# Two rows of a down-projection at once, a rotation product on another engine, and a fourth weight pair, in an encoder layer on one Trainium2 core

## The chip, the cores and the metric

The kernel runs on one core of one Trainium2 chip. The metric is the device time of one execution in microseconds (us); lower is better. A core has five engines that work side by side, each through its own queue in order: TensorE (PE in the profile, its weight loads PEld), VectorE (DVE), ScalarE (ACT), GpSimd (POOL) and SyncE (SP), which here only issues transfers.

## The reference

One layer of an encoder on 512 tokens of width 1024, all in 32-bit floats:

```python
def swiglu(x, w1, w3, w2):
    return (jax.nn.silu(x @ w1) * (x @ w3)) @ w2          # 1024 -> 2816 -> 1024

def layer(x):
    x = x + 0.5 * swiglu(rmsnorm(x, ffn1_norm), ...)
    h = rmsnorm(x, mix_norm)
    proj = h @ w_in                # queries, keys, values of attentions A and B, gates
    o_a = dilated attention of three head groups with a T5 position bias, merged
    q, k = rope(rmsnorm(q, q_norm)), rope(rmsnorm(k, k_norm))   # attention B, 8 heads of 128, 2 of k and v
    o_b = softmax(q @ k.T * scale) @ v
    x = x + (sigmoid(g_a) * (o_a @ P_a) + sigmoid(g_b) * (o_b @ P_b)) @ w_out
    x = x + 0.5 * swiglu(rmsnorm(x, ffn2_norm), ...)
    return rmsnorm(x, final_norm)

def apply_rope(x, cos, sin):       # on pairs of columns
    return x0 * c - x1 * s, x0 * s + x1 * c
```

## The kernel before

The activations lie transposed: 8 tiles of 128 features x 512 tokens (`x`). Each matmul of 32-bit numbers is made of three on split operands (`mm3`, L215 to L217): a high part `H` and a rest `L` of each side, as H·H, H·L and L·H. So each weight tile of 128x1024 is loaded by SP (`wr`, `wa`, `wt`), cast by ScalarE to its high part (`wh`, L200) and subtracted by VectorE for the rest (`wl`, L201): it is "split". The order in which all weight tiles are used is one list (`self.order`). Before each use, `weights` issues the loads and splits ahead of it, as far as buffers go: three pairs `wh`, `wl` (the ring "wh"), and, while a pool `self.wx` is open, a fourth pair (the ring "whx") for every fourth tile of some kinds. A pair is free again when TensorE has done its last matmul with it.

TensorE's instructions run in the order in which the code writes them (`manual_schedule`); the other engines' queues are put in order by the tile scheduler. A static queue runs in order on the chip, so a row that waits holds those behind it.

The stages that the change touches:

- *FFN* (`ffn_run`, twice, "a" and "b"). The hidden 22 tiles are made in three groups (8, 8, 6 columns of tiles) by a Strassen scheme, two tiles at a time; the last step of a pair is `A22`, then VectorE multiplies (`c`, L459, L460) and the result `gg` is cast (ScalarE, L424) and its rest formed (VectorE, L425). After each group comes a down-projection with `w2` (`blocks`): for each of 8 output rows, one bank of PSUM collects the products with all `gg` of the group (24 matmuls for eight, 18 for six), and is added to `x` (`add`, L479 and L480). Four banks `mm` go round. In the first group of the first FFN, `done` of rows 0 to 2 also calls `bias_rows`: SP loads `onehot` and `vmask` (one buffer each), TensorE makes a small product `bps` (L579), VectorE makes `v` (L580), and GpSimd writes it out.
- *Rope stage of attention B*. The projections ("b", 0), ("b", 1), ("b", 2) take four banks at once, one per 128 tokens, and use 12 weight tiles `wb`; gate row ("g", 8) stands between the last two. For each 128 tokens `rope` copies the bank (`xk`, ScalarE), squares it (`sqb`), sums (`ss`, VectorE) and gets 1/root (`ms`, VectorE; `rs`, GpSimd, L365); `turn`, one step later, scales `xk` (L910), forms the product with the cosines `xa` on VectorE (L911) and with the sines `xb` on GpSimd (L912), and combines them on VectorE (L913, L914). `rope_t` transposes `xk` on TensorE (`Tq`) for the attention, which follows with scores `Sb`, exponentials `Pb`, transposes `Tb` and `PTH`, `PTL`. A gate row leaves its bank through VectorE (`z`, L617).

Of the kernel before, what the change touches and what calls it, by code (L numbers as in the profile page):

```python
# [28 lines left out]
GAP_S = 2  # L29
GAP_B = 1  # L30
LAG = 1
T = 512
D = 1024
NK = 8
# [16 lines left out]
def tile_at(li):  # L51
    if li < 4:
        return 256 * li, (256 if li < 3 else 128), (0 if li < 3 else 64)
    return GP + 256 * (li - 4), 256, 256


def f32(t):
    return t.bitcast(F32)


class Layer:
# [123 lines left out]
    def prep(self):  # L185
        n = len(self.tiles)
        if n == len(self.order) or not (n in self.raws or self.kind[n] == "ws"):
            return False
        tag = "whx" if self.order[n][0][:2] in ("sw", "w2") and n % 4 == 3 and self.wx is not None else "wh"
        both = self.ring(tag, n, self.used, n)  # L190
        if both is None:
            return False
        name, key = self.order[n][:2]
        if n not in self.raws:
            self.load(n)
        raw, (H, L) = self.raws[n], both
        if name[:2] == "sw" and key[1] in ("S2", "S4"):
            a, b = (self.raws[self.index[name, (key[0], q)]] for q in (("S1", "A11") if key[1] == "S2" else ("S2", "A12")))
            self.nc.vector.tensor_add(raw, a, b)
        self.nc.scalar.copy(H, raw)  # L200
        self.nc.vector.tensor_sub(L, raw, f32(H))  # L201
        self.tiles.append(both)
        return True
# [123 lines left out]
        s = slice(128 * (n % 8), 128 * (n % 8) + 128)  # L327
        return self.cur[0][:, s], self.cur[1][:, s]

    def blocks(self, name, rows, n=0):  # L330
        for pairs, done in rows:
            ps = self.bank()
            for k, pair in enumerate(pairs):
                self.mm3(ps, *self.block(name, n), *pair, k == 0, k == len(pairs) - 1)
                n += 1
            done(ps)

    @staticmethod
    def weave(main, fill):
# [63 lines left out]
    def ffn_run(self, s, gin, gnext, hooks, out, side, gp):  # L403
        nc = self.nc
        g, t, c, half = [], {}, {}, []
# [96 lines left out]
        lo, n = first, 0  # L502
        for gi, hi in enumerate(ends):
            last = hi == NF
            for _ in self.strassen(s, range(lo, hi, 2), evict):
                for fn in late[:2]:
                    fn()
                del late[:2]

            def done(d, ps, gi=gi, last=last):  # L510
                down(d, ps, last)
                if (gi, d) in side:
                    side[gi, d]()

            rows = [(list(g), lambda ps, d=d: done(d, ps)) for d in range(NK)]
            if last and out is not None:
                break
            self.blocks("w2" + s, rows, n)
            n, lo = n + NK * len(g), hi
            g.clear()  # L520
        if out is None:
            return
        nf, half = len(g), NK // 2
        self.blocks("w2" + s, rows[:half], n)
        ws = [[self.block("w2" + s, n + d * nf + f) for f in range(nf)] for d in range(half, NK)]

        def norm(hf):
# [13 lines left out]
        for hf in range(2):  # L541
            cs = slice(256 * hf, 256 * hf + 256)
            for d in range(half, NK):
                ps = self.bank()
# [354 lines left out]
    def turn(self):  # L899
        if self.turned is None:  # L900
            return
        (grp, i, nh, xk, rs), self.turned = self.turned, None
        nc, bp = self.nc, self.bp
        GC, GS = self.tabs[1 if grp == 0 else 0]
        w = 128 * nh
        x4 = xk[:, :w].rearrange("p (h e d) -> p h e d", h=nh, e=2)
        bc = lambda t: t[:, i].unsqueeze(1).to_broadcast([128, nh, 2, 64])
        xa = bp.tile([128, 4, 2, 64], F32, tag="xa", name="xa", bufs=2)[:, :nh]
        xb = bp.tile([128, 4, 2, 64], F32, tag="xb", name="xb", bufs=2)[:, :nh]
        nc.vector.tensor_mul(x4, x4, rs[:, :nh].unsqueeze(2).unsqueeze(3).to_broadcast([128, nh, 2, 64]))  # L910
        nc.vector.tensor_mul(xa, x4, bc(GC))  # L911
        nc.gpsimd.tensor_mul(xb, x4, bc(GS))  # L912
        nc.vector.tensor_sub(x4[:, :, 0], xa[:, :, 0], xb[:, :, 1])  # L913
        nc.vector.tensor_add(x4[:, :, 1], xb[:, :, 0], xa[:, :, 1])  # L914
        self.roped[grp, i] = xk
# [64 lines left out]
    def mixer(self):  # L980
        nc, tc = self.nc, self.tc
# [6 lines left out]
        with tc.tile_pool(name="oA", bufs=1, reuse_waits="tile") as oa:  # L988
# [25 lines left out]
            with tc.tile_pool(name="B", bufs=1, reuse_waits="tile") as bp:  # L1014
                self.qH = bp.tile([128, 8, T], F32R, name="qH")
                self.qL = bp.tile([128, 8, T], F32R, name="qL")
                with tc.tile_pool(name="KV", bufs=1, reuse_waits="tile") as kv:
                    self.kH = kv.tile([128, 2, T], F32R, name="kH")
                    self.kL = kv.tile([128, 2, T], F32R, name="kL")
                    self.vH = kv.tile([128, 4, 256], F32R, name="vH")  # L1020
                    self.vL = kv.tile([128, 4, 256], F32R, name="vL")
                    with tc.tile_pool(name="Bp", bufs=1, reuse_waits="tile") as b2:
                        self.rope_tables(b2)
                        self.until(fill, ("b", 0))
                        self.weave(self.rope_t(0, 4, 4), fill)
                        self.until(fill, ("b", 1))
                        self.weave(self.rope_t(1, 6, 6), fill)
                        self.until(fill, ("b", 2))
                        self.weave(self.rope_t(2, 6, 4), fill)
                    with tc.tile_pool(name="Ba", bufs=2, reuse_waits="tile") as pp:  # L1030
                        self.weave(self.attn_b(pp), fill)
                for _ in fill:
                    pass
                self.hctx.close()
                with tc.tile_pool(name="M", bufs=1, reuse_waits="tile") as mp:
                    mH = [mp.tile([128, T], F32R, name=f"mH{d}") for d in range(NK)]
                    mL = [mp.tile([128, T], F32R, name=f"mL{d}") for d in range(NK)]
                    m = {}

                    def gate(j):  # L1040
                        z = mp.tile([128, T], F32, tag="z", name="zg", bufs=4)
                        nc.sync.dma_start(z, self.gate_d[j])
                        nc.scalar.activation(z, z, AF.Sigmoid, bias=self.par[:, G_BG + j:G_BG + j + 1])
                        return z

                    def done_a(d, ps):
                        m[d] = mp.tile([128, T], F32, tag="ma", name="ma", bufs=2)
                        nc.vector.tensor_mul(m[d], ps, gate(d))

                    def done_b(d, ps):  # L1050
                        z = gate(NK + d)
                        nc.vector.tensor_mul(z, ps, z)
                        nc.vector.tensor_add(z, z, m[d])
                        nc.scalar.copy(mH[d], z)
                        nc.vector.tensor_sub(mL[d], z, f32(mH[d]))

                    def done_o(d, ps):
                        nc.vector.tensor_add(self.x[d], self.x[d], ps)
                        self.norm_h(d, G_FFN2)
                        self.norm_sq(d)  # L1060

                    oa_p = list(zip(self.oH, self.oL))
                    ob_p = [(self.qH[:, k, :], self.qL[:, k, :]) for k in range(8)]
                    rows = []
                    for d in range(NK):
                        rows += [(oa_p, lambda ps, d=d: done_a(d, ps)), (ob_p, lambda ps, d=d: done_b(d, ps))]
                    self.blocks("wab", rows)
                    self.open_h()
                    mm = list(zip(mH, mL))
                    self.blocks("wo", [(mm, lambda ps, d=d: done_o(d, ps)) for d in range(NK)])  # L1070
# [64 lines left out]
    return w.reshape(k // 128, 128, n // 128, 128).transpose(2, 1, 0, 3).reshape(n // 128, 128, k)  # L1135


def block_chunks(w):
    k, n = w.shape
    b = w.reshape(k // 128, 128, n // 128, 128).transpose(2, 0, 1, 3).reshape(-1, 8, 128, 128)  # L1140
    return b.transpose(0, 2, 1, 3).reshape(-1, 128, 1024)


# [5 lines left out]
def arrange(inp):  # L1149
    p = {k: np.asarray(v) for k, v in inp.items()}  # L1150
    out = constants()
# [6 lines left out]
    half = np.concatenate([np.arange(0, 128, 2), np.arange(1, 128, 2)])  # L1158
    gqk = np.stack([p["q_norm"][0][half], p["k_norm"][0][half]]).reshape(1, 2, 2, 64)
    out["gqk"] = np.broadcast_to(gqk, (128, 2, 2, 64))  # L1160
    for s, n in (("a", 1), ("b", 2)):
        w1 = feat_chunks(p[f"ffn{n}_w1"][0])
        w3 = feat_chunks(p[f"ffn{n}_w3"][0])
        out["w13" + s] = np.stack([w1, w3], axis=1).reshape(2 * NF, 128, 1024)
        ends = (0,) + GROUPS[s][1:]
        w2 = p[f"ffn{n}_w2"][0]
        out["w2" + s] = np.concatenate([block_chunks(w2[128 * lo:128 * hi]) for lo, hi in zip(ends, ends[1:])])
    w = p["w_in"][0]
    wa = w[:, :4608].reshape(D, 3, 3, 512)
    qk = wa[:, 0:2].reshape(D, 2, 3, 4, 128)  # L1170
# [28 lines left out]
```

## Time and profile before

| | |
|---|---|
| median of 3 runs | 1311.01 us (1309.3 to 1313.32) |
| profiled execution | 1314.01 us, its span 1312.2 us |
| mean granted TensorE clock | 0.993 |
| TensorE, VectorE, ScalarE, GpSimd busy | 97%, 67%, 45%, 11% of the span |
| DMA | 181.91 MB, mean 139 GB/s |

A row of the profile's timeline reads: start in us from the span's start, duration in us, engine, line, operation, output<-inputs by the program's names, shapes, count, and in brackets the idle time of the engine before it with what ended that. Of a row in a view of waits: who waited <- for whom: us in total, times, the longest. A matmul's row lasts longer than the distance to the next, since they are pipelined; the distance of two starts is what one takes of the time.

### The profile page before, as it was taken

Reading aid. Unit: us, or ns where it says so; the run is one execution under the profiler, and the core shown is the slowest. Engines: PE = TensorE matmul, PEld = TensorE weight load, DVE = VectorE, ACT = ScalarE, POOL = GpSimd, SP = SyncE. Lnnn points to the kernel's source line nnn. Section 1 sums busy time; section 2 is a strip of 40 time slices with the busy share of each in tenths; the row PEclk is TensorE's granted clock in tenths of the full one; section 3 lists DMA queues with packets and bytes.
Section 4 is the critical chain, followed back from the end, with each engine's and each line's share of the span. In section 5 each row is a group of like instructions: output and inputs, shape, how many; then the busy total and the mean of one; then the engine's idle time right before and its main releaser. Section 6 shows DMA issues by size and latency. Waiting matters only on the chain.

```text
span 1312.2 us, 19971 instructions
## 1 busy us (share of the span) xinstructions
PE 1277.0 (97%) x7994; PEld 1124.2 (86%) x7994; DVE 881.6 (67%) x1322; ACT 589.4 (45%) x883; POOL 144.5 (11%) x140
## 2 busy tenths in 40 slices
PE   8999999999999999999998999999999999999997
PEld 6897999899789999877876778888889889988986
DVE  7884688468674785666466598655577747775775
ACT  7551354145453443644233455643475315442553
POOL 3111110000211112100023300000301000100001
PEclk9999999999999999999998999999999999999998
DMA  7875776352375757532222221345637536653321
GB/s 232 240 190 168 173 195 175 96 129 80 115 193 138 207 165 249 156 101 83 92 97 75 71 74 40 105 161 168 198 97 183 166 90 178 160 168 96 99 80 65
DMA packets 85549, 181.91 MB, mean 139 GB/s; under 512 B 12480, under 2 KB 19024, under 8 KB 85456
## 3 DMA queue, kind: packets, MB, share of 16 engines
q1 hardware_dynamic: 67904, 140.74, 32.7%
q0 software_dynamic: 16832, 39.34, 15.0%
q8 instruction: 63, 1.03, 0.4%
q10 hardware_dynamic: 720, 0.55, 0.1%
q14 instruction: 30, 0.25, 0.1%
HBM read 168.98 MB, written 15.29 MB: 140 GB/s over the span
## 4 chain that ended last, share of the span: by engine, by line
PE 80%; DVE 8%; DMA 5%; issue 4%; ACT 2%; POOL 1%; SPq 0%; POOLq 0%; DVEq 0%; ACTq 0%
PE mm L215 21%; PE mm L216 21%; PE mm L217 21%; PE Y L215 3%; PE Y L216 3%; PE Y L217 3%; DVE wl L201 2%; DMA wt<-in_waq 2%; PE X L215 1%; PE X L217 1%; PE X L216 1%; PE Tb L955 1%; PE S L765 1%; PE mm L816 1%; DMA wr<-in_w2b 1%
## 5 line engine op out<-in xcount | busy, mean ns | idle before, releaser
L200 ACT CAST wh<-wr 128x1024 fp32r<-128x1024 f32 x142 | 148.7, 1048 | 246.1 <-PE mm L216 149.3
L201 DVE TENSOR_TENSOR wl<-wr,wh 128x1024 fp32r<-128x1024 f32 x142 | 174.1, 1226 | 57.6 <-ACT wh L200 57.5
L215 PE MATMUL mm<-hH,wh 128*128 128x256 f32 (+1 forms) x600 | 201.1, 335 | 4.9 <-ACT wh L1086 4.9
L217 PE MATMUL mm<-hH,wl 128*128 128x256 f32 (+1 forms) x600 | 197.5, 329 | 0.8 <-DVE wl L201 0.5
L216 PE MATMUL mm<-hL,wh 128*128 128x256 f32 (+1 forms) x600 | 197.1, 329 | 0.7 <-DVE hL L348 0.7
L216 PE MATMUL mm<-gg,wh 128*128 128x512 f32 (+1 forms) x376 | 143.8, 382 | 3.6 <-DVE gg L425 3.6
L215 PE MATMUL mm<-gg,wh 128*128 128x512 f32 (+1 forms) x376 | 144.0, 383 | 0.7 <-ACT gg L424 0.6
L217 PE MATMUL mm<-gg,wl 128*128 128x512 f32 (+1 forms) x376 | 143.2, 381 | 0.0
L215 PEld LDWEIGHTS mm<-hH,wh 128*128 128x128 f32 x600 | 113.4, 189 | 18.2 <-ACT wh L1086 4.9
L217 PEld LDWEIGHTS mm<-hH,wl 128*128 128x128 f32 x600 | 113.3, 189 | 12.6 <-DVE wl L201 0.9
L216 PEld LDWEIGHTS mm<-hL,wh 128*128 128x128 f32 x600 | 113.3, 189 | 11.8 <-DVE hL L348 2.1
L479 DVE TENSOR_TENSOR u<-mm,R 128x512 f32<-128x512 f32 (+1 forms) x52 | 33.8, 650 | 98.3 <-PE mm L217 98.2
L200 ACT CAST wh<-wa 128x1024 fp32r<-128x1024 f32 x48 | 50.4, 1050 | 101.3 <-PE mm L216 48.3
L216 PEld LDWEIGHTS mm<-gg,wh 128*128 128x128 f32 x376 | 71.1, 189 | 19.2 <-DVE gg L425 5.4
L215 PE MATMUL mm<-TH,wh 128*128 128x256 f32 x304 | 84.9, 279 | 2.6 <-DVE c L451 2.6
L215 PEld LDWEIGHTS mm<-gg,wh 128*128 128x128 f32 x376 | 71.2, 189 | 17.3 <-ACT gg L424 2.0
L217 PE MATMUL mm<-TH,wl 128*128 128x256 f32 x304 | 84.8, 279 | 0.1
L215 PE MATMUL mm<-wh,hH 128*128 128x512 f32 x192 | 79.6, 414 | 5.5 <-DVE z L617 5.0
L216 PE MATMUL mm<-TL,wh 128*128 128x256 f32 x304 | 84.7, 279 | 0.0
L217 PEld LDWEIGHTS mm<-gg,wl 128*128 128x128 f32 x376 | 71.2, 189 | 14.1
L200 ACT CAST wh<-ws 128x1024 fp32r<-128x1024 f32 x48 | 50.4, 1050 | 70.3 <-PE mm L216 52.7
L201 DVE TENSOR_TENSOR wl<-wt,wh 128x1024 fp32r<-128x1024 f32 x48 | 58.6, 1221 | 33.4 <-ACT wh L200 33.2
(230 smaller groups left out, 3176.1 us busy)
## 6 DMA issues: line engine op xcount, KB each, us to landing
wr<-in_w2a SPq DMA_DIRECT2D x22, 512.0 KB, 3.5
wr<-in_w2b SPq DMA_DIRECT2D x22, 512.0 KB, 3.5
wt<-in_w13b SPq DMA_DIRECT2D x20, 512.0 KB, 4.2
wa<-in_w13b SPq DMA_DIRECT2D x20, 512.0 KB, 4.1
wt<-in_w13b POOLq DMA_DIRECT2D x20, 512.0 KB, 6.0
wt<-in_w13a SPq DMA_DIRECT2D x18, 512.0 KB, 3.6
wt<-in_w13a POOLq DMA_DIRECT2D x18, 512.0 KB, 6.1
wa<-in_w13a SPq DMA_DIRECT2D x18, 512.0 KB, 3.6
```

What stands on the lines that cost most here:

```text
L200: self.nc.scalar.copy(H, raw)
L201: self.nc.vector.tensor_sub(L, raw, f32(H))
L215: mm(out, lH, rH, start=start, stop=False, skip_group_check=more)
L216: mm(out, lH, rL, start=False, stop=False, skip_group_check=more)
L217: mm(out, lL, rH, start=False, stop=stop, skip_group_check=more)
L479: nc.vector.tensor_mul(u, ps, R)
L765: nc.tensor.matmul(*args, start=True, stop=True)
L816: nc.tensor.matmul(oc, v, p, start=st, stop=sp)
L955: nc.tensor.transpose(pt[:, 128 * j:128 * j + 128], P[h, j][:, 128 * k:128 * k + 128], self.ident)
```

## The change

Three edits. `blocks` gets a `lag`: for the down-projections (LAST = 2) the first two output rows take two banks and are computed together, each first without its last two blocks, then the last two of row 0, then of row 1; the host lays the `w2` blocks out in the same order (`sequence`, `block_chunks`). The product `xb` moves from GpSimd to VectorE. And during the rope stage `self.wx` is that stage's pool, so that every fourth `wb` tile has the fourth pair.

```diff
+LAST = 2
+def sequence(sizes, lag):
+    head = sizes[:2] if lag else []
+    return ([(r, k) for r, m in enumerate(head) for k in range(m - lag)] + [(r, k) for r, m in enumerate(head) for k in range(m - lag, m)]
+            + [(r, k) for r, m in enumerate(sizes) if r >= len(head) for k in range(m)])
...
-        tag = "whx" if self.order[n][0][:2] in ("sw", "w2") and n % 4 == 3 and self.wx is not None else "wh"
+        tag = "whx" if self.order[n][0][:2] in ("sw", "w2", "wb") and n % 4 == 3 and self.wx is not None else "wh"
...
-    def blocks(self, name, rows, n=0):
-        for pairs, done in rows:
-            ps = self.bank()
-            for k, pair in enumerate(pairs):
-                self.mm3(ps, *self.block(name, n), *pair, k == 0, k == len(pairs) - 1)
-                n += 1
-            done(ps)
+    def blocks(self, name, rows, n=0, lag=0):
+        banks = {}
+        for r, k in sequence([len(pairs) for pairs, _ in rows], lag):
+            pairs, done = rows[r]
+            if k == 0:
+                banks[r] = self.bank()
+            self.mm3(banks[r], *self.block(name, n), *pairs[k], k == 0, k == len(pairs) - 1)
+            n += 1
+            if k == len(pairs) - 1:
+                done(banks.pop(r))
...
-            self.blocks("w2" + s, rows, n)
+            self.blocks("w2" + s, rows, n, LAST)
...
-        self.blocks("w2" + s, rows[:half], n)
+        self.blocks("w2" + s, rows[:half], n, LAST)
...
-        nc.gpsimd.tensor_mul(xb, x4, bc(GS))
+        nc.vector.tensor_mul(xb, x4, bc(GS))
...
                         self.rope_tables(b2)
+                        self.wx = b2
                         self.until(fill, ("b", 0))
...
+                    self.wx = None
...
-def block_chunks(w):
+def block_chunks(w, lag=0):
     k, n = w.shape
-    b = w.reshape(k // 128, 128, n // 128, 128).transpose(2, 0, 1, 3).reshape(-1, 8, 128, 128)
+    b = w.reshape(k // 128, 128, n // 128, 128).transpose(2, 0, 1, 3)
+    b = np.stack([b[r, c] for r, c in sequence([k // 128] * (n // 128), lag)]).reshape(-1, 8, 128, 128)
```

Lines that the diff adds shift the numbers: L215 to L217 are L222 to L224 after, L200 and L201 L207 and L208, L424 and L425 L434 and L435, L479 L489, L579 L589, L617 L627, L912 L922.

The order on TensorE at the second down-projection of the first FFN, before (`mm_2234` is the bank of row 0, `mm_2269` of row 1; `gg_2231` holds the last pair of columns of the group):

```order
L217 MATMUL mm_2234<-gg_2097,wl_2133 128x512
L215 MATMUL mm_2234<-gg_2231,wh_2132 128x512
...
L217 MATMUL mm_2234<-gg_2231,wl_2133 128x512
L215 MATMUL mm_2269<-gg_1644,wh_2163 128x512
L216 MATMUL mm_2269<-gg_1644,wh_2163 128x512
```

After (`mm_2259` is now row 1's bank):

```order
L224 MATMUL mm_2234<-gg_2097,wl_2133 128x512
L222 MATMUL mm_2259<-gg_1644,wh_2132 128x512
...
L224 MATMUL mm_2259<-gg_2097,wl_2164 128x512
L222 MATMUL mm_2234<-gg_2231,wh_2163 128x512
...
L224 MATMUL mm_2234<-gg_2231,wl_2164 128x512
L222 MATMUL mm_2259<-gg_2231,wh_2163 128x512
```

Row 1's first six blocks now stand between row 0's first six and the first matmul that reads the last pair of `gg`.

TensorE around the bias products in the first down-projection of all, after (`mm_1011` and `mm_1036` are rows 0 and 1; before, the 24 matmuls of the whole of row 1 stand between the same two `bps`):

```order
L224 MATMUL mm_1011<-gg_1008,wl_941 128x512
L589 MATMUL bps_1087<-onehot_1082,rel_bias_172 8x383
L222 MATMUL mm_1036<-gg_1008,wh_940 128x512
...
L224 MATMUL mm_1036<-gg_1008,wl_941 128x512
L589 MATMUL bps_1105<-onehot_1100,rel_bias_172 8x255
```

The two `bps` stand six matmuls apart. SP's queue at the same place, before and after in one piece each, first before:

```order
L169 DMA wr<-in_w2a 128x1024 x5
L577 DMA onehot<-in_onehot 32x255
L577 DMA vmask<-in_vmask 8x255
L169 DMA wr<-in_w2a 128x1024
L577 DMA onehot<-in_onehot 32x255
L577 DMA vmask<-in_vmask 8x255
L179 DMA wr<-in_w13a 128x2x512 x3
```

And after:

```order
L176 DMA wr<-in_w2a 128x1024 x6
L587 DMA onehot<-in_onehot 32x255
L587 DMA vmask<-in_vmask 8x255
L587 DMA onehot<-in_onehot 32x255
L186 DMA wr<-in_w13a 128x2x512
L587 DMA vmask<-in_vmask 8x255
L186 DMA wr<-in_w13a 128x2x512 x2
```

All `w2` loads now stand ahead of the reloads of `onehot`, and the loads of the next phase among them.

VectorE at the end of the second rope burst, up to the gate row `z`, before (the third and fourth turn; `wl` is the split of a weight tile):

```order
L201 TENSOR_TENSOR wl<-wr,wh 128x1024
L893 TENSOR_REDUCE ss<-sqb 128x4
L911 TENSOR_TENSOR xa<-xk,GC_6379 128x512
L364 TENSOR_SCALAR ms<-ss 128x4
L913 TENSOR_TENSOR xk<-xa,xb 128x4x64
L914 TENSOR_TENSOR xk<-xb,xa 128x4x64
L910 TENSOR_TENSOR xk<-xk,rs 128x512
...
L932 TENSOR_TENSOR qL<-Tq,qH 128x4x128
...
L617 TENSOR_TENSOR z<-mm,R 128x512
```

After:

```order
L903 TENSOR_REDUCE ss<-sqb 128x4
L921 TENSOR_TENSOR xa<-xk,GC_6379 128x512
L374 TENSOR_SCALAR ms<-ss 128x4
L922 TENSOR_TENSOR xb<-xk,GS_6380 128x512
L920 TENSOR_TENSOR xk<-xk,rs 128x512
...
L208 TENSOR_TENSOR wl<-wr,wh 128x1024
L923 TENSOR_TENSOR xk<-xa,xb 128x4x64
L924 TENSOR_TENSOR xk<-xb,xa 128x4x64
L942 TENSOR_TENSOR qL<-Tq,qH 128x4x128
L627 TENSOR_TENSOR z<-mm,R 128x512
```

`xb` stands on VectorE in each turn, the split that stood ahead of the fourth turn's sums now stands behind its products, and `z` still comes behind all four turns and the first `qL`. In the third burst the same engine has one split among the turns instead of two; the one that is missing there stands ahead of the first burst.

More of the change, by code (lines that the diff above doesn't have):

```diff
@@ L1166, in arrange @@
         w2 = p[f"ffn{n}_w2"][0]
-        out["w2" + s] = np.concatenate([block_chunks(w2[128 * lo:128 * hi]) for lo, hi in zip(ends, ends[1:])])
+        out["w2" + s] = np.concatenate([block_chunks(w2[128 * lo:128 * hi], LAST) for lo, hi in zip(ends, ends[1:])])
     w = p["w_in"][0]
```

## The prediction

> **What bounds the kernel now.** I read the page first, then the waits of TensorE alone (largest in total first), then TensorE's and VectorE's rows in order of time around the longest of them. TensorE is busy for 97% of the span, so only its idle moments can be won; the second view names them (total us, times, longest).
>
> ```profile
> PE 1277.0 (97%) x7994; PEld 1124.2 (86%) x7994; DVE 881.6 (67%) x1322; ACT 589.4 (45%) x883; POOL 144.5 (11%) x140
> ```
>
> ```profile
> PE mm L215 <- DVE z L617: 5.0, 1, 5.0
> ...
> PE mm L216 <- DVE gg L425: 3.6, 5, 1.0
> ...
> PE Tb L955 <- DVE Pb L949: 1.8, 2, 1.3
> ```
>
> The change aims at three of these: `gg` (the last gated columns before a down-projection, 5 times), `z` (one wait in the rope stage) and what follows the rope stage (`Pb`). A stall costs more than its idle time, and can cost the clock too. TensorE at the `gg` stall of the second FFN's first down-projection, then four stretches of time (length; busy time and instructions of TensorE, its weight loads, VectorE, ScalarE and GpSimd; granted clock; DMA share and GB/s):
>
> ```profile
> 1038.57 0.39 PE L216 MATMUL mm<-gg,wh 128*128 128x512 f32 x1
> 1038.80 0.40 PE L217 MATMUL mm<-gg,wl 128*128 128x512 f32 x1
> 1039.78 0.49 PE L215 MATMUL mm<-gg,wh 128*128 128x512 f32 x1 [0.58 <-ACT gg L424]
> 1041.23 0.50 PE L216 MATMUL mm<-gg,wh 128*128 128x512 f32 x1 [0.95 <-DVE gg L425]
> 1041.57 0.39 PE L217 MATMUL mm<-gg,wl 128*128 128x512 f32 x1
> ...
> 1042.53 0.63 PE L217 MATMUL mm<-gg,wl 128*128 128x512 f32 x1
> 1042.95 0.63 PE L215 MATMUL mm<-gg,wh 128*128 128x512 f32 x1
> ```
>
> ```profile
> 714.30:721.00 6.70, 5.61 (x13) 4.45 (x14) 3.99 (x6) 1.04 (x1) 0.00 (x0) 0.50 0.34 120
> 1038.50:1041.90 3.40, 1.86 (x7) 0.99 (x7) 2.36 (x2) 1.23 (x2) 0.00 (x0) 1.00 0.43 145
> 1042.00:1045.30 3.30, 3.30 (x9) 2.52 (x8) 2.08 (x3) 1.04 (x1) 0.00 (x0) 0.50 0.20 82
> 1158.00:1161.30 3.30, 1.85 (x16) 1.89 (x17) 3.27 (x5) 1.05 (x1) 0.00 (x0) 1.00 1.03 210
> ```
>
> Start to start a 128x512 matmul takes 0.23 us (1038.57 to 1038.80). Across the first stall it is 0.98, so 0.75 lost for 0.58 idle (0.17 more); across the second 1.45, then 0.34, so 1.33 for 0.95 idle (0.38 more). In the 3.4 us from 1038.5 TensorE was busy for 1.86, and after them the clock is granted at 0.50 for 3.3 us, with a start every 0.42: 3.3 x (1 - 0.23/0.42) = 1.5 us more. From 1158.0 it was busy for 1.85 of 3.3, and the clock stayed: the line lies near 45% idle.
>
> **Part 1, the first two rows of each down-projection together.** Before, the last pair of columns is needed after the other blocks of one row; now after those of two. With eight blocks that is six blocks x three matmuls x 0.23 = 4.1 us later, with six (the last group of each FFN) 2.7 us. The worst stall above is 0.75 + 1.33 = 2.1 us, so all five end. The gain is 3.6 us of idle, 5 x 0.38, the 0.75 above and 1.5 of clock: 7.8 us. Late next would be a weight tile, but the fourth of this projection is split at 1038.81 and the second is needed only 5.5 us after the start at about 1034.7; the others are split earlier:
>
> ```profile
> 1038.81 1.23 DVE L201 TENSOR_TENSOR wl<-wr,wh 128x1024 fp32r<-128x1024 f32 x1 [1.61 <-ACT wh L200]
> ```
>
> The number of matmuls, evictions and bytes is the same. Rows 0 and 1 are evicted 4.1 and 0 us later, close together; VectorE idles between these rows, and four banks leave room. But in the first group of the first FFN, finishing a row also issues a bias matmul, whose `onehot` tile has one buffer. Its rows, SP's reload, and the landing time of this tile's three loads after issue (least/median/most):
>
> ```profile
> 100.72 0.81 PE L579 MATMUL bps<-onehot,rel_bias 32*8 32x383 f32 x2
> 107.15 0.59 PE L579 MATMUL bps<-onehot,rel_bias 32*8 32x255 f32 x2
> ```
>
> ```profile
> 101.56 0.33 SPq L577 DMA_DIRECT2D onehot<-in_onehot  x1
> ```
>
> ```profile
> DMA to landing us min/median/max: 1.7/5.2/8.8
> ```
>
> The reload is issued 0.84 us after the bias matmul starts (101.56 less 100.72) and lands 1.7 us later at best, 2.5 in all. Before, 6.4 us lie between the two bias matmuls; now only six matmuls do, 0.74 (100.72 to the next start) + 1.4 = 2.1 us. So TensorE waits 0.4 us at least; a sixth `w2` load may still be on the rings, and at 8.8 the wait is 7.5. I take 0.5, near the least, since here the weight loads come 5.5 us apart. SP holds a first load of the next phase (`wr`, an A22 tile) behind the third `onehot`, and two more behind a `vmask`; both releases come with the second row, earlier than VectorE frees their buffers. Part 1: 7.3 us.
>
> **Part 2, the second rotation product on VectorE, and part 3, the fourth pair.** The rope rows of the second projection group, VectorE and then GpSimd:
>
> ```profile
> 700.15 0.69 DVE L910 TENSOR_TENSOR xk<-xk,rs 128x512 f32<-128x512 f32 x1 [1.12 <-POOL rs L365]
> 700.87 0.69 DVE L911 TENSOR_TENSOR xa<-xk,GC 128x512 f32<-128x512 f32 x1
> 702.75 0.42 DVE L913 TENSOR_TENSOR xk<-xa,xb 128x256 f32<-128x256 f32 x1 [1.19 <-POOL xb L912]
> ...
> 708.78 1.20 DVE L911 TENSOR_TENSOR xa<-xk,GC 128x512 f32<-128x512 f32 x1
> ...
> 712.13 0.69 DVE L911 TENSOR_TENSOR xa<-xk,GC 128x512 f32<-128x512 f32 x1
> 712.74 0.68 DVE L932 TENSOR_TENSOR qL<-Tq,qH 128x512 fp32r<-128x512 f32 x1
> 713.97 0.42 DVE L913 TENSOR_TENSOR xk<-xa,xb 128x256 f32<-128x256 f32 x1 [0.55 <-POOL xb L912]
> ...
> 714.65 0.68 DVE L617 TENSOR_TENSOR z<-mm,R 128x512 f32<-128x512 f32 x1
> ```
>
> ```profile
> 707.28 2.15 POOL L912 TENSOR_TENSOR xb<-xk,GS 128x512 f32<-128x512 f32 x1 [0.87 <-DVE xk L910]
> ```
>
> ```profile
> 709.97 0.40 PE L217 MATMUL mm<-wh,hL 128*128 128x512 f32 x1
> 715.39 0.80 PE L215 MATMUL mm<-wh,hH 128*128 128x512 f32 x1 [5.03 <-DVE z L617]
> ```
>
> TensorE's next matmul needs the bank of the ninth gate row, which `z` frees; `z` stands in VectorE's queue behind four turns. It still does in the new order, so the stall shrinks by what the turns shrink. A product on VectorE is priced by `xa`, the same form: 0.69 us, 0.61 to the next independent start (712.13 to 712.74); its ends are that and the 1.20 of 708.78, which overlaps GpSimd's `xb`. Removed: waits for `xb` of 1.19 in each of the first two turns and 0.55 in the fourth (2.9), and 0.5 of that overlap; added 4 x 0.61 = 2.4. Laid out row by row with these starts (a split 1.14, GpSimd's `rs` as it was), the new order also lets rows of the next turn fill the waits for `rs` (1.12 each) and the gaps behind dependent rows (700.15 to 700.87 is 0.72): about 1.4. The second `xk` then starts at 699.05, and `z` at 712.2, 2.4 us earlier; the bounds are 0.0 (products at 1.20) and 3.5 (all waits for `rs` filled in the second to fourth turn). The stall falls from 5.2 to 2.8. The clock was 0.50 from 714.3 to 721; TensorE ran at it from 715.39, 5.6 us x 0.45 = 2.5 lost. By the line at 45% of 3.4 us, a hole of 2.8 us takes it down unless it is cut in the middle, now for one such stretch rather than two: 1.2 lost (0 to 2.5). This stall gains 2.4 + 1.3 = 3.7.
>
> The fourth pair moves each `wb` split one tile ahead: two splits stay in this burst, but of the next burst's two, one goes to an earlier, idle place. A split holds VectorE 1.14 us. There the turns shrink by 2.3 + 1.1 = 3.4 us, and with them what TensorE waits for behind it (the first row belongs to the first burst):
>
> ```profile
> 680.65 0.50 PE L215 MATMUL mm<-wh,hH 128*128 128x512 f32 x1 [0.46 <-DVE vL L889]
> ...
> 752.44 0.63 PE L928 MATMUL Tq<-ident,xk 128*128 128x128 f32 x4 [0.55 <-DVE xk L914]
> ...
> 754.68 0.50 PE L215 MATMUL Sb<-kH,qH 128*128 128x512 f32 x1 [0.23 <-DVE qL L932]
> ```
>
> With the surcharges `Tq` and `Sb` cost 0.7 and 0.5; the two `Pb` waits (1.8 idle, in the attention right behind) 2.1. Those two end. `Pb` hangs on VectorE's chain of maxima, which starts up to 3 us sooner, but then waits for the scores; I credit 1.5, in all 2.7 (1.2 to 3.3). At 680.65, in the first burst, the idle of 0.46 ends, since a 0.43 product and a split no longer stand ahead of it: 0.8. GpSimd keeps the small powers, and its loads are untouched.
>
> **Sum.** 7.3 + 3.7 + 2.7 + 0.8 = 14.5 us. The profiled execution took 1314.0 us (span 1312.2, 1.8 around it), 3.0 above the median of 1311.0. Part of that may be the clock's 4.0 us (1.5 and 2.5), which would then be less to win in the median; I take 0.5 off: 1311.0 - 14.0 = 1297.0.
>
> **Rivals.** (a) The clock stays up in the rope hole: 1.2 more, 1295.8; with the hole at its least (`z` 3.5 us earlier, not 2.4), 1294.7. The Trainium skill, TensorE: Matmul & The Clock Gate, section HAM oscillation, gives the rule "no PE-idle gaps >~3.4µs", by which a hole of 2.8 us would keep the full clock and the sum be 1295.8. The trace disagrees: two holes of 0.58 and 0.95 us took it to 0.50 at 1042. Chance 0.2. (b) The rope part gives nothing: the products cost 1.20, `z` and `Pb` stay; 1297 + 7 = 1304. Against it: 1.20 only appears beside GpSimd's product, which goes. 0.16. (c) The FFN gain is given back: TensorE comes earlier to phases whose loads set the pace (all of part 1): 1304. Against it: those loads start when TensorE's own reads free a buffer, so they move too. 0.08. (d) The `onehot` reload lands at 8.8 us: 7 more and one window of clock, 1305.5. 0.05. (e) Slower: the same wait, but the reload queued behind several weight loads; from 14 us after issue it eats the whole gain, at 18 it gives 1315. Against it: its SP neighbours land by then. 0.03. (f) Nothing moves: the stalls pass to the next release, 1311. 0.03. Forecast 0.45.
>
> **How the numbers follow.** About 0.3%, 3.9 us, is what a measurement here tells from no change, so faster is below 1307.1. Forecast and (a) to (d) lie there, 0.94; parts of (b), (c) and (d) could coincide, so I give 0.90, same 0.07, slower 0.03. The likeliest case alone spans 1294.7 (a) to 1299.8 (clock lost as before, `Pb` not credited); the range takes in (b), (c) and (d): 1292 to 1306.
>
> **What would show it.** `gg` gone from TensorE's waits, and no window of clock 0.50 near 1042 (part 1); a short new wait for the second `bps` near 107; the `z` wait 2.6 us idle rather than 5.0, `xb` on VectorE at 0.69 and no `xa` at 1.20; `Pb` and `Tq` waits under 1 us together. It is wrong if another wait stands where `gg` stood, if `z` is no earlier, or if the reload lands late.

## The result, and the profile after

| | median, us | runs | before beside it | ratio, 95% interval |
|---|---|---|---|---|
| changed kernel | 1297.94 | 4 (1296.20 to 1298.46) | 1312.16 | 0.9892 [0.9871, 0.9913] |
| changed kernel, measured again beside the experiments | 1300.13 | 6 (1295.37 to 1302.29) | 1309.38 | 0.9917 [0.9892, 0.9942] |

The change makes the kernel faster by 14.2 us in the first measurement (11.4 to 16.9) and by 10.9 in the second (7.6 to 14.1). Predicted were 14.0 less and 1297.0, range 1292 to 1306; both medians lie in the range. The first profiled execution of the changed kernel took 1298.5 us (span 1296.7). First the page's line of busy times, then the waits of TensorE (line waited for; total us, times, longest):

```profile
PE 1270.6 (98%) x7994; PEld 1123.2 (87%) x7994; DVE 885.3 (68%) x1334; ACT 588.9 (45%) x883; POOL 125.9 (10%) x128
```

```profile
PE mm L222 <- DVE z L627: 3.4, 1, 3.4
PE mm L222 <- DVE c L461: 2.5, 2, 1.6
...
PE Tb L965 <- DVE Pb L959: 0.6, 1, 0.6
...
PE bps L589 <- DMA onehot<-in_onehot: 0.4, 1, 0.4
```

GpSimd lost the 12 products and VectorE gained them. No line names `gg`, `Tq`, `Sb` or `vL` any more; `Pb` fell from 1.8 to 0.6; `z` fell from 5.0 to 3.4 rather than to 2.6; and the new wait of the second `bps` is there. TensorE's rows at that new wait and at `z`, in order of time (start, us, instruction, idle before and its releaser):

```profile
107.02 0.40 PE L224 MATMUL mm<-gg,wl 128*128 128x512 f32 x1
107.78 0.59 PE L589 MATMUL bps<-onehot,rel_bias 32*8 32x255 f32 x2 [0.36 <-DMA onehot<-in_onehot]
```

```profile
709.51 0.79 PE L222 MATMUL mm<-wh,hH 128*128 128x512 f32 x1 [3.35 <-DVE z L627]
710.10 0.63 PE L223 MATMUL mm<-wl,hH 128*128 128x512 f32 x1
```

Start to start, the first costs 0.76 instead of 0.23, so 0.53. The rows that set `z`, VectorE's and then GpSimd's:

```profile
688.70 0.69 DVE L903 TENSOR_REDUCE ss<-sqb 128x4 f32<-128x512 f32 x1 [1.73 <-ACT sqb L901]
...
690.77 0.69 DVE L920 TENSOR_TENSOR xk<-xk,rs 128x512 f32<-128x512 f32 x1 [1.19 <-POOL rs L375]
691.50 0.69 DVE L921 TENSOR_TENSOR xa<-xk,GC 128x512 f32<-128x512 f32 x1
692.11 0.68 DVE L922 TENSOR_TENSOR xb<-xk,GS 128x512 f32<-128x512 f32 x1
...
695.03 0.69 DVE L920 TENSOR_TENSOR xk<-xk,rs 128x512 f32<-128x512 f32 x1 [0.90 <-POOL rs L375]
...
700.42 0.69 DVE L920 TENSOR_TENSOR xk<-xk,rs 128x512 f32<-128x512 f32 x1 [0.90 <-POOL rs L375]
...
703.88 0.69 DVE L920 TENSOR_TENSOR xk<-xk,rs 128x512 f32<-128x512 f32 x1 [0.90 <-POOL rs L375]
...
708.77 0.68 DVE L627 TENSOR_TENSOR z<-mm,R 128x512 f32<-128x512 f32 x1
```

```profile
693.95 1.05 POOL L375 TENSOR_TENSOR rs<-ms,mhalf 128x4 f32<-128x4 f32 x1 [3.21 <-DVE ms L374]
699.01 1.38 POOL L375 TENSOR_TENSOR rs<-ms,mhalf 128x4 f32<-128x4 f32 x1 [4.01 <-DVE ms L374]
702.54 1.31 POOL L375 TENSOR_TENSOR rs<-ms,mhalf 128x4 f32<-128x4 f32 x1 [2.15 <-DVE ms L374]
```

The products are as priced (0.69 and 0.68, 0.61 from start to start), and no wait for `xb` is left. From the first sum to `z` the burst takes 20.07 us (688.70 to 708.77); before it took 21.80, from this row to `z` at 714.65:

```profile
692.85 0.69 DVE L893 TENSOR_REDUCE ss<-sqb 128x4 f32<-128x512 f32 x1 [1.81 <-ACT sqb L891]
```

What VectorE waits for now is `rs` alone, in every turn.

### The profile page after: what moved, and what is told of

Its sections match the earlier page's. It is cut to its first block, busy times and chain, and to the rows that moved or that the text cites. A ratio compares the mean times of both kernels' runs of the same rounds, so it can differ in the third digit from the quotient of the medians.

```text
span 1296.7 us, 19953 instructions
## 1 busy us (share of the span) xinstructions
PE 1270.6 (98%) x7994; PEld 1123.2 (87%) x7994; DVE 885.3 (68%) x1334; ACT 588.9 (45%) x883; POOL 125.9 (10%) x128
## 4 chain that ended last, share of the span: by engine, by line
PE 86%; DVE 7%; issue 3%; DMA 2%; ACT 1%; POOL 1%; SPq 0%; POOLq 0%; DVEq 0%; ACTq 0%
PE mm L222 22%; PE mm L224 22%; PE mm L223 22%; PE Y L222 3%; PE Y L224 3%; PE Y L223 3%; DVE wl L208 2%; PE X L222 2%; PE X L224 1%; PE X L223 1%; PE Tb L965 1%; PE S L775 1%; PE mm L826 1%; PE T L844 1%; DMA d<-SO 1%
## 5 line engine op out<-in xcount | busy, mean ns | idle before, releaser
L207 ACT CAST wh<-wr 128x1024 fp32r<-128x1024 f32 x142 | 148.7, 1048 | 235.6 <-PE mm L223 142.7
L208 DVE TENSOR_TENSOR wl<-wr,wh 128x1024 fp32r<-128x1024 f32 x142 | 173.4, 1221 | 64.1 <-ACT wh L207 63.9
L222 PE MATMUL mm<-hH,wh 128*128 128x256 f32 (+1 forms) x600 | 200.8, 335 | 4.9 <-ACT wh L1098 4.9
L224 PE MATMUL mm<-hH,wl 128*128 128x256 f32 (+1 forms) x600 | 197.2, 329 | 1.4 <-DVE wl L1099 0.9
L222 PE MATMUL mm<-gg,wh 128*128 128x512 f32 (+1 forms) x376 | 143.1, 381 | 0.0
L224 PE MATMUL mm<-gg,wl 128*128 128x512 f32 (+1 forms) x376 | 142.6, 379 | 0.0
L222 PEld LDWEIGHTS mm<-hH,wh 128*128 128x128 f32 x600 | 113.3, 189 | 18.0 <-ACT wh L1098 4.9
L224 PEld LDWEIGHTS mm<-hH,wl 128*128 128x128 f32 x600 | 113.0, 188 | 13.1 <-DVE wl L1099 1.2
L207 ACT CAST wh<-wa 128x1024 fp32r<-128x1024 f32 x48 | 50.4, 1050 | 101.6 <-PE mm L223 49.9
L489 DVE TENSOR_TENSOR u<-mm,R 128x512 f32<-128x512 f32 (+1 forms) x52 | 33.8, 650 | 85.2 <-PE mm L224 85.0
L222 PE MATMUL mm<-TH,wh 128*128 128x256 f32 x304 | 84.9, 279 | 2.5 <-DVE c L461 2.5
L224 PE MATMUL mm<-TH,wl 128*128 128x256 f32 x304 | 84.7, 279 | 0.0
L222 PEld LDWEIGHTS mm<-gg,wh 128*128 128x128 f32 x376 | 70.8, 188 | 15.2 <-issue 1.1
L224 PEld LDWEIGHTS mm<-gg,wl 128*128 128x128 f32 x376 | 70.8, 188 | 14.2
L222 PE MATMUL mm<-wh,hH 128*128 128x512 f32 x192 | 79.3, 413 | 3.4 <-DVE z L627 3.4
L207 ACT CAST wh<-ws 128x1024 fp32r<-128x1024 f32 x48 | 50.4, 1051 | 69.5 <-PE mm L223 51.7
L208 DVE TENSOR_TENSOR wl<-wt,wh 128x1024 fp32r<-128x1024 f32 x48 | 58.7, 1223 | 33.7 <-ACT wh L207 33.4
```

Of the source, the lines that this page charges most:

```text
L222: mm(out, lH, rH, start=start, stop=False, skip_group_check=more)
L224: mm(out, lL, rH, start=False, stop=stop, skip_group_check=more)
L489: nc.vector.tensor_mul(u, ps, R)
```

## The experiments

Each kernel is compared with the kernel before, run beside it on the same chip. The median of the kernel before was 1310.4 us beside rows alone, product alone, pair alone and changed and bank; 1309.4 beside changed again, product and pair, bank alone and the second `onehot`; 1309.5 beside no power. The gain in us is one less the ratio, times that median. The ratio is not the quotient of the two medians: by the medians changed again gains 9.3, product and pair 5.0, bank alone 7.6, changed and bank 17.7, no power 15.3, and the others differ from the table by less than 1 us. All of these lie within the intervals.

| kernel | ratio, 95% interval | gain, us | idle of the `z` wait, us | half-rate windows behind it | lost there, us |
|---|---|---|---|---|---|
| before, first profile | 1 | | 5.03 | 2 | 8.0 |
| rows alone | 0.9967 [0.9953, 0.9981] | 4.3 | 5.02 | 2 | 8.0 |
| product alone | 0.9952 [0.9936, 0.9968] | 6.3 | 2.91 | 1 | 4.9 |
| pair alone | 1.0008 [0.9998, 1.0018] | -1.0 | 5.12 | 2 | 8.0 |
| product and pair | 0.9952 [0.9933, 0.9971] | 6.3 | 3.35 | 0 | 3.5 |
| changed, first profile | 0.9892 [0.9871, 0.9913] | 14.2 | 3.35 | 2 | 6.3 |
| changed, again | 0.9917 [0.9892, 0.9942] | 10.9 | 3.01 | 1 | 4.7 |
| bank alone | 0.9932 [0.9911, 0.9953] | 8.9 | none | 0 | 0 |
| changed and bank | 0.9875 [0.9856, 0.9894] | 16.4 | none | 0 | 0 |
| changed, bank, second `onehot` | 0.9874 [0.9851, 0.9898] | 16.5 | none | 0 | 0 |
| changed, no power | 0.9863 [0.9825, 0.9900] | 17.9 | none | 0 | 0 |

The last column is what TensorE's starts between 690 and 735 us take beyond the usual (median) distance of matmuls of the same shape, in one execution each. A half-rate window is a stretch of 3.41 us in which the clock is granted at 0.50.

**Rows alone, product alone, pair alone.** Each is one part of the diff put into the kernel before: `LAST` with `sequence` and the weights' order; then the two lines

```
-        nc.gpsimd.tensor_mul(xb, x4, bc(GS))
+        nc.vector.tensor_mul(xb, x4, bc(GS))
```

```
-        tag = "whx" if self.order[n][0][:2] in ("sw", "w2") ...
+        tag = "whx" if self.order[n][0][:2] in ("sw", "w2", "wb") ...
```

the latter with `self.wx` set around the rope stage. (In rows alone it stays set too, but no tile of that stage uses it there; the starts from 690 to 735 and from 735 to 800 us lose 8.0 and 4.6 us, about as before, 8.0 and 4.7.) Expected of the rows:

> Part 1 alone (rows 0 and 1 of each down-projection together; the second product stays on GpSimd, no fourth pair for the second attention's projections). Theory (the parts add up by stage): the five gg waits go and a wait of about 0.4 us for the second bps comes; 7.4 us less than before, 1304.5 to 1305; the z wait stays at 5.0, Pb at 1.8, and the clock is granted at 0.50 only once inside the span, near 710. Rival 1 (the stalls of 0.7 us near 453, 473 and 474, which the changed kernel lost without a word of the prediction on them, end because of part 1): 1.7 more, about 1303. Rival 2 (part 1 does not pay by itself, the later phases wait for what TensorE now reaches earlier): under 5 us.

Measured 4.3 us (2.5 to 6.2). The `gg` waits are gone, the `bps` wait is 0.3, `z` and `Pb` are as before, as the theory says; the time is not. The stalls near 473 stayed (0.84 and 0.57 idle); the one at 453 is missing, but it is missing in the product alone too, where part 1 is not; rival 1 falls. Rival 2 named under 5 us, and the number fits it, but not its reason: the waits that grew most are one for `wl`, from 0.3 to 0.9 us, and one for `c`, from 0.5 to 0.8, while another for `c` fell from 2.6 to 1.2. Why 4.3 and not 7.4 is read from the other kernels that keep the rows in turn. Their waits for `gg`, in the order product alone, product and pair, bank alone:

```profile
PE mm L216 <- DVE gg L425: 2.6, 4, 0.8
```

```profile
PE mm L216 <- DVE gg L425: 3.1, 5, 0.8
```

```profile
PE mm L216 <- DVE gg L425: 3.2, 4, 1.0
```

The code around `gg` is the same in all of them, and so it is in the pair alone, where the line reads 2.6 again. The first profile of before had 3.6 and 0.6 more on ScalarE. By starts, the five executions with the rows in turn lose 5.7, 3.8, 3.7, 5.4 and 5.2 us to `gg`, on average 4.8; the clock fell behind it in two of the five, for 1.5 each, 0.6 on average; the new `bps` wait takes 0.5. That makes 4.9, which the measured interval holds. The one profile that the prediction had was the most costly draw of five.

Of the product, and of the pair:

> The second rotation product on VectorE alone (rows in turn, no fourth pair). Theory: the z wait falls from 5.0 to 3.4, with the clock at 0.50 for 6.8 us behind it as before (two windows), since one split and the powers at 1.0 to 1.4 stay; 1.7 us there, about 1.5 in the third burst and 0.5 at vL: 3 to 4 us less than before, about 1308.5. Rival 1 (the fourth pair carries the gain in the bursts, because the product only moves work onto the engine that TensorE waits for): under 1.5 us, and vL and Pb waits stay. Rival 2 (the prediction's own sizes): the z wait 2.6 and one window of clock, 3.7 there.

> The fourth weight pair for the second attention's projections alone (the product stays on GpSimd). Theory: it moves a split of 1.1 us out of the third burst to an earlier place; vL's wait of 0.5 goes, Pb falls by about 1 us, z stays within 0.5 of 5.0: 1 to 2 us less than before, about 1310.5. Rival 1: it does nothing alone, since GpSimd's product sets the pace of the turns: within 0.5 us. Rival 2: the earlier split collides with GpSimd's product and z comes later: up to 1 us more than before.

The product alone gains 6.3 us (4.2 to 8.4), more than the 3 to 4 expected, and rival 1 (under 1.5) falls; with 2.91 us idle and one half-rate window, `z` came out near rival 2. From the first sum to `z` its burst takes 19.74 us, about as in the changed kernel, and `vL`, `Tq` and `Sb` no longer wait. The pair alone gains nothing (between 0.3 faster and 2.4 slower) where 1 to 2 us were expected, and `vL` still waits 0.6. Its third rope burst has one split less than before and is still longer: from the first sum to the `z` behind it 22.77 us instead of 21.83. VectorE at the third and fourth turn, pair alone:

```profile
744.08 0.42 DVE L914 TENSOR_TENSOR xk<-xb,xa 128x256 f32<-128x256 f32 x1
744.42 1.22 DVE L201 TENSOR_TENSOR wl<-wr,wh 128x1024 fp32r<-128x1024 f32 x1
745.56 0.68 DVE L893 TENSOR_REDUCE ss<-sqb 128x4 f32<-128x512 f32 x1
...
747.56 0.69 DVE L910 TENSOR_TENSOR xk<-xk,rs 128x512 f32<-128x512 f32 x1 [1.12 <-POOL rs L365]
748.29 0.69 DVE L911 TENSOR_TENSOR xa<-xk,GC 128x512 f32<-128x512 f32 x1
750.16 0.42 DVE L913 TENSOR_TENSOR xk<-xa,xb 128x256 f32<-128x256 f32 x1 [1.18 <-POOL xb L912]
```

And before:

```profile
743.96 0.69 DVE L910 TENSOR_TENSOR xk<-xk,rs 128x512 f32<-128x512 f32 x1 [1.12 <-POOL rs L365]
744.57 1.22 DVE L201 TENSOR_TENSOR wl<-wr,wh 128x1024 fp32r<-128x1024 f32 x1
745.71 0.68 DVE L893 TENSOR_REDUCE ss<-sqb 128x4 f32<-128x512 f32 x1
```

Before, a split and the fourth turn's sums stand inside the third turn, where VectorE would wait for GpSimd's product. Without that split the order lets the third turn end first, and the fourth runs alone with its whole waits of 1.12 and 1.18. So the split had been covered, and the pair uncovered the wait. With the product on VectorE there is no such wait to fill, and the same pair shortens this burst from 19.74 (product alone) to 18.78 us (changed kernel).

**The parts together.**

> The changed kernel itself, measured beside the three below. The parts measured alone gave 0.9967 (rows), 0.9952 (product) and 1.0008 (pair), which add up to 9.6 us. Theory A (the first pair of medians flattered it; the parts add, and the pair is worth 0.7 with the product on VectorE because the wait for Pb falls from 1.3 to 0.6): 10 to 11.5 us less than before. Theory B (the parts help each other, since a stall more or less moves the next one): 13 us or more less, as first measured.

> Parts 2 and 3 without part 1 (product on VectorE and the fourth pair, rows in turn). Theory: 0.7 us less than the product alone (0.9952), so 6 to 7.5 us less than before: about 0.9948; third burst's Tq and Sb waits gone, Pb 0.6. Rival (the pair only pays where part 1 has moved TensorE): no better than the product alone.

The second is the changed kernel with `sequence` and `LAST` taken out. The changed kernel measured again gives 10.9 us, product and pair 6.3: rows add 4.3 to them (1304.43 less 1300.13), as much as alone, and 4.3 + 6.3 is 10.6. So the parts add up, as theory A has it (10 to 11.5 for the whole; by the medians it is 9.3); the interval of the whole, 7.6 to 14.1, leaves room for two or three us that come only when the parts stand together. In time the pair cannot be told from nothing (0.9952 with it and without); in the waits it brings `Pb` from 1.3 to 0.6.

**The clock behind the `z` wait.** Stretches of 3.4 us on the edges at which the granted clock changes (us, then busy time and instructions of TensorE, its weight loads, VectorE, ScalarE, GpSimd; granted clock; DMA share, GB/s): the changed kernel's first profile, the changed kernel again, then product and pair.

```profile
705.44:708.86 3.42, 0.72 (x4) 0.24 (x2) 3.42 (x7) 0.59 (x1) 0.00 (x0) 1.00 0.08 18
708.86:712.27 3.41, 2.76 (x7) 2.18 (x8) 2.33 (x3) 0.00 (x0) 0.00 (x0) 0.50 0.77 250
712.27:715.68 3.41, 3.41 (x10) 2.63 (x9) 1.22 (x1) 1.04 (x1) 0.00 (x0) 0.50 0.33 124
```

```profile
708.10:711.52 3.42, 0.48 (x3) 0.04 (x1) 3.42 (x7) 0.41 (x1) 0.00 (x0) 1.00 0.24 75
711.52:714.93 3.41, 3.34 (x8) 2.66 (x9) 1.75 (x3) 0.37 (x1) 0.00 (x0) 0.50 0.78 272
714.93:718.35 3.42, 3.42 (x19) 2.79 (x18) 1.62 (x2) 1.26 (x2) 0.00 (x0) 1.00 0.23 73
```

```profile
709.88:713.30 3.42, 1.84 (x11) 1.18 (x9) 3.42 (x7) 0.59 (x1) 0.00 (x0) 1.00 0.01 2
713.30:716.71 3.41, 1.64 (x7) 1.37 (x8) 3.41 (x6) 0.00 (x0) 0.00 (x0) 1.00 0.64 224
716.71:720.12 3.41, 3.41 (x19) 2.78 (x18) 1.46 (x3) 1.64 (x2) 0.00 (x0) 1.00 0.54 163
```

In all three the hole is 3.0 or 3.35 us long. In the third an edge cuts it into 1.58 and 1.77, and the clock stays up: 3.5 lost. In the second it lies in one window and ends within 0.07 of the edge: one half-rate window, 4.7 lost. In the first, 2.70 lie in one window and 0.65 in the next; the window at half rate that was idle for these 0.65 us is followed by another: 6.3 lost. So a wait of about this length cost 0, 1.4 or 2.9 us of clock in these executions by where the edges fell, and that differs from execution to execution. The hole of 5.0 before covered a whole window in each profile (from 710.83 in the first), and took two half-rate windows each time.

**Another bank for the ninth gate row.** The remaining stall is taken away at its root: TensorE waits for `z` only because its next row needs the bank that `z` reads.

```
-    def feat(self, name, n, done):
-        ps = self.bank()
+    def feat(self, name, n, done, aside=False):
+        ps = self.aux("zb") if aside else self.bank()
...
-                yield from self.feat("wg", n, done)
+                yield from self.feat("wg", n, done, n == 8)
```

On the changed kernel, and alone on the kernel before:

> The changed kernel, with the ninth gate row computed in a bank of the other pool of PSUM, so that TensorE's next row does not wait for z to free its bank. Theory (the clock falls only because TensorE stands idle for 3.4 us here): the z wait of 3.4 and the 2.9 us at half clock both go, 6.3 us less than the changed kernel, about 1291.5, and no 0.50 inside the span. Rival 1 (VectorE is late by the same amount for whatever comes next): another wait of 2 to 3 us stands within 10 us of the place, under 2 us won. Rival 2 (the hole is cut but the clock falls all the same): the wait goes, the 0.50 stays, about 3.5 won, 1294.5.

> The kernel before, with only the ninth gate row in a bank of the other pool (rows in turn, product on GpSimd, no fourth pair). Theory: the z wait of 5.0 us and the 2.9 us at half clock behind it go, since the row behind z needs nothing else of VectorE within 5 us: 7 to 8 us less than before, about 1303. Rival 1 (VectorE, 1.7 us later than in the changed kernel, is late with the split that comes behind z, so TensorE waits there): a wl wait of 1 to 3 us in its place, 4 to 6 less. Rival 2 (the gain of the whole change in this stage is only what the bank gives): then this equals the bank's gain on the changed kernel, 5 to 6.

On the changed kernel, VectorE's `z` (now `zb`) and a window around it:

```profile
708.88 0.68 DVE L627 TENSOR_TENSOR z<-zb,R 128x512 f32<-128x512 f32 x1
```

```profile
705.00:710.00 5.00, 5.00 (x26) 4.00 (x25) 5.00 (x10) 1.64 (x2) 0.00 (x0) 1.00 0.27 85
```

`z` is as late as before the edit, and TensorE is busy throughout at the full clock. The kernel takes 1292.75 us, 16.4 less than before (13.9 to 18.9); the theory said 1291.5, and rivals 1 and 2, a wait passed on or a clock that falls all the same, are not seen. The theory's 6.3 us less than the changed kernel is 2.2 by that kernel's first measurement and 5.5 by its second. Alone the bank gains 8.9 us (6.2 to 11.7) at three changed lines, where 7 to 8 were expected, and no `wl` wait takes the place of `z`. That is the largest gain of a single edit here, though its interval overlaps that of the product alone, 6.3 (4.2 to 8.4).

**Two buffers for `onehot` besides.**

```
-            t[k] = self.bp.tile([p, V0], F32, tag=k, name=k)[:, :n]
+            t[k] = self.bp.tile([p, V0], F32, tag=k, name=k, bufs=2 if k == "onehot" else 1)[:, :n]
```

> The changed kernel with the ninth gate row in a bank of the other pool and with two buffers for onehot. Theory: the wait of 0.3 to 0.4 us for the second bps goes too, 0.5 less than with the bank alone (1292.75), no 0.50 of the clock inside the span in most runs: about 1292. Rival (the earlier onehot reload pushes weight loads back on SP): no gain, or a new wait for wl in the first FFN.

The `bps` wait is gone, but the time (1293.82 us, 0.9874) cannot be told from that with the bank alone: half a microsecond is below what these runs separate. In this profile the clock fell once, behind a wait of 2.5 us for `PT` in the first attention that none of these edits touches, as in bank alone and in the changed kernel again. Both versions gain more than the changed kernel as measured again (16.4 and 16.5 us against 10.9), but cannot be told from its first measurement (14.2); the one with the bank alone is enough.

**What is left of the `z` wait.** The power is left out, and with it GpSimd from the turns:

```
-        self.rpow(rs[:, :nh], ss[:, :nh], 1.0 / HD_B)
+        nc.vector.tensor_scalar(rs[:, :nh], ss[:, :nh], 1.0 / HD_B, EPS, op0=ALU.mult, op1=ALU.add)
```

> The changed kernel without the power in the rope stage: the small factor rs is the scaled sum itself, written by VectorE, so the root and GpSimd's part in the turns are left out. Theory (what is left of the z stall is VectorE waiting four times for GpSimd's rs, 1.19 + 3 x 0.90 us in the changed kernel's trace, against about 0.15 for a dependent row on VectorE): z comes about 3 us earlier, the z wait falls from 3.4 to 0.5 or less and takes no clock with it; 4 to 6 us less than the changed kernel, about 0.988 of before. Rival (the products and the splits set z, the waits for rs are filled): the z wait stays above 2 us.

VectorE at the first factor, and at `z`:

```profile
690.91 0.69 DVE L903 TENSOR_REDUCE ss<-sqb 128x4 f32<-128x512 f32 x1 [1.73 <-ACT sqb L901]
691.63 0.17 DVE L905 TENSOR_SCALAR rs<-ss 128x4 f32<-128x4 f32 x1
691.84 0.69 DVE L920 TENSOR_TENSOR xk<-xk,rs 128x512 f32<-128x512 f32 x1
...
706.87 0.68 DVE L627 TENSOR_TENSOR z<-mm,R 128x512 f32<-128x512 f32 x1
```

From the first sum to `z` it is 15.96 us, 4.1 less than in the changed kernel's first profile, with the products and splits in place; `z` no longer stalls TensorE, the clock stays at 1.00, and the kernel takes 1294.19 us. So what bounds the burst after the change is the round trip to GpSimd for `rs`, four times about 1 us. This kernel's gain is no offer, since it computes another factor.

## Why the prediction was right, and where its terms were not

- **Part 1, 7.3 us; measured 4.3, alone and on top of the other two.** The mechanism was right: all five stalls ended, no 0.50 stood near 1042 in the profiles of the changed kernel, and `bps` waited 0.5 as taken. The mis-sized term is the gross 7.8, read off one execution as if its stalls were fixed. Five executions average 5.4 with the clock. The 0.5 that the prediction took off for the profile's being above the median was too little by about two.
- **Stall at `z`, 3.7 us (2.4 earlier, 1.3 of clock).** `z` came 1.73 us earlier in the first profile and 2.07 when measured again: the failed step is "GpSimd's `rs` as it was". The four powers of the burst took 1.01, 1.01, 1.01 and 1.24 us before, and 1.01, 1.05, 1.38 and 1.31 in the changed kernel's first profile (1.05 for the third when measured again), while VectorE ran rows with two inputs beside the last three. From the start of `ms` to the start of the scaling that needs `rs`, the four turns together took 5.37 us before, 6.11 after and 5.77 when measured again. These 0.74 and 0.40 us more are about the 0.7 and 0.3 that are missing from the 2.4. The clock step, "one such stretch rather than two", is wrong as a rule and near the truth as a mean: four executions with the product gave 2, 1, 1 and 0. Their mean loss is 4.85 against 8.0 before, a gain of 3.1.
- **Third burst 2.7, `vL` 0.8.** `Tq`, `Sb` and `vL` waits ended and `Pb` fell to 0.6, as said; the starts between 735 and 800 us lose 1.6 instead of 4.7 (3.1). The prediction credited one sum to both parts; product alone carries 2.2 of it, the pair the rest, and alone the pair would have lost.
- **The sum, 14.0.** By stages it is 4.3 + 3.1 + 3.1 + 0.6 = 11.1, close to the 10.9 of the second measurement. The first, 14.2, agrees with 14.0 partly by chance: in that profile the stages that the change does not touch were cheap too (the starts between 440 and 500 us lost 1.4 us, 2.4 when measured again; those between 500 and 650 lost about 4 and 6). When measured again the clock also fell once more, at 1148 us, behind a wait of 2.1 us for `c` in the second FFN; product alone shows such a fall behind the same wait, so part 1 is not needed for it.
- **Rivals.** (a), the clock stays up: seen once in four executions, with a hole of 3.35, by a cut in the middle, which the text had named as the exception. The Trainium skill, TensorE: Matmul & The Clock Gate, section What's actually happening, calls the window free-running, 3413 ns; the edges here agree: the stretches at 0.50 last one or two times 3.41 us, and their edges fall at other places in the three executions shown above. The same page's rule of no idle gaps over about 3.4 us, in its section HAM oscillation, does not decide here: holes of 2.91 and 3.01 us took the clock down, and of two of 3.35 one did not. (b) to (f): `z` and `Pb` moved, no later wait grew to the size of what was won, the reload cost 0.5; none held.

## What to carry to other kernels

A stall in one profile is a draw: where the same code is run in several kernels, compare the same wait in all of them before its size goes into a sum, and price the clock by the length of the hole and the chance of where the window's edges fall, not by one profile. Before shortening the work ahead of a late row, ask what TensorE really needs from it: here it was a bank, and another bank alone gave 8.9 us, where the faster rope (product and pair) gave 6.3. A row that is moved away may have been filling a wait; look at what stands in its place.

## What the runs showed of the hardware that was not expected

- The line for the clock is not in idle time alone. Windows with TensorE busy for 1.84 and 1.64 us (product and pair, above) and for 1.60 kept it, windows with 1.87 lost it (that of before at 1038.51, and the first of these two pairs, product and pair again; the second is the changed kernel with the bank):

```profile
225.19:228.60 3.41, 1.87 (x7) 1.21 (x7) 2.13 (x2) 0.90 (x1) 0.00 (x0) 1.00 0.76 261
228.60:232.02 3.42, 3.42 (x9) 2.69 (x9) 2.52 (x3) 1.04 (x1) 0.00 (x0) 0.50 0.04 17
```

```profile
560.02:563.43 3.41, 1.60 (x21) 1.36 (x21) 1.20 (x6) 0.53 (x2) 0.00 (x0) 1.00 0.59 155
563.43:566.85 3.42, 3.38 (x20) 2.35 (x16) 3.32 (x14) 1.23 (x2) 0.00 (x0) 1.00 0.21 85
```

  Both that fell at 1.87 held two holes, each with a slow restart behind it; those that kept the clock at less held one. At the very end of the span, where matmuls of 128x1 stand in the window, it fell even at 2.15 (product alone, from 1292.57; no power, from 1280.31). What the monitor counts stays open.
- A window at half rate that is itself idle for 0.65 to 1.15 us did not bring the clock back: 1.15 in before, 1.06 in rows alone, 0.85 in pair alone, 0.65 in the changed kernel's first profile. One idle for 0.07 or less did, in all 14 such windows of these profiles.
- A power on GpSimd takes longer beside a VectorE row with two inputs. Of 128x4 it took 1.01 us wherever VectorE stood idle, and 1.05 to 1.38 beside such rows. Why the third of the second burst took 1.05 in three executions and 1.38 in three others, beside the same rows, stays open. In the first burst one of 128x2 took 0.70 us alone and 1.80 beside the split of a weight tile, as here in before (GpSimd's row, then VectorE's), and so in all four profiles with `xb` on GpSimd:

```profile
681.28 1.80 POOL L365 TENSOR_TENSOR rs<-ms,mhalf 128x2 f32<-128x2 f32 x1 [2.17 <-DVE ms L364]
```

```profile
681.31 1.21 DVE L201 TENSOR_TENSOR wl<-wr,wh 128x1024 fp32r<-128x1024 f32 x1
```

  The Trainium skill, SBUF — State Buffer, section Who interferes with whom, says that a VectorE instruction with two SBUF inputs contends with a GpSimd instruction that reads SBUF. These rows agree, and the price here lay between 0.04 and 1.1 us.
